# First block: the column groups of the modulation issued together, scores on a head's own rows, values of two heads at once, a split step-size weight

## The chip, the core and the metric

The program runs on one core of one Trainium2 chip. The metric is device time in microseconds, the median of several runs. The core has TensorE (PE, matmuls, with its weight loads listed apart as PEld), VectorE (DVE), ScalarE (ACT), GpSimd (POOL) and SyncE (SP), which here only issues DMA loads. Each engine works through its own instruction list in order; semaphores tie the lists together.

## The reference, cut to what matters

Two transformer blocks follow each other, each with a mixture of experts. The change lies in the first block alone. There a conditioning vector makes shifts, scales and gates (the modulation), and four mixers work beside each other on 256 tokens (and 256 context tokens): neighbourhood attention, a gated delta rule in both directions, differential attention and a Fourier mix.

```python
m_lat = jnp.split((s_lat @ w_mod[l] + b_mod[l])[:, None, :], 6, axis=-1)
h_lat = modulate(rmsnorm(x_lat, norm1_g[l]), m_lat[0], m_lat[1])
...
(na_q, na_k, na_v, dn_qkv, dn_a, dn_b, dn_gate, df_q, df_k, df_v, ft_u) = split_proj(h_lat @ w_in)
...
def diff_core(q, k, v, lam):
    s = jnp.einsum('bqhmd,bkhmd->bhmqk', q, k).astype(F32) * q.shape[-1] ** -0.5
    p = jax.nn.softmax(s, axis=-1)
    a = p[:, :, 0] - lam * p[:, :, 1]
    return jnp.einsum('bhqk,bkhd->bqhd', a, v.astype(F32))
...
x_lat = x_lat + m_lat[2] * (mix_lat @ w_out[l])
x_lat = x_lat + m_lat[5] * expert_choice_ffn(h_lat, w_router[l], w_gate[l], w_up[l], w_down[l])
```

Four heads of differential attention have two score maps each, over 32 features a map; a head's values have 64 features. `dn_a` and `dn_b` are the delta rule's step sizes, 16 columns of `w_in`. The second block has a modulation weight of its own, `w_mod_2`, which depends on no token and is worked off in the first block.

## The kernel before, in words

**Order.** A tile framework decides at build time in which order each engine's list stands; a generator `yield`s an estimate of the work it has just written. `beside(a, b, share)` mixes two generators, `weave(chain, fill)` writes a serial chain with another generator's pieces in between. A scheduler then places instructions by priorities and readiness, so the order of a list is not that of the code.

**Stages of the first block.** 1. The norm and the first 2048 columns of the modulation (`mods`, set 0). 2. Projections, the step sizes (`abp`, `abt`), the convolutions and the decay factors. 3. `solve()`, a triangular solve on DVE, one row of X after another, and woven into it the rest of the projections (`pj`, three fp32r products of high and low halves each) beside `mods` sets 1 and 2 of `w_mod`. What is left of that fill after the solve goes on alone. 4. `delta()`, the delta rule over 16 steps (state products `pa`, `oi`, `pb`, and `uw` for each new pair of steps), with `neighbours()`, `difference()`, `fourier()` and the three sets of `w_mod_2` woven in. 5. What is left of these, then the out-projection `pw` with `w_out`, router and experts.

**Modulation.** `mods` loads eight chunks of 1 MB of a set (tile `wmod`, from `S.load`'s ring of four buffers; 11 more are there once pool `main` is closed). For each it issues four matmuls with a 32-column stationary, each on its own column group, so that four groups fill the array. Their sums stand in one PSUM tile `mp` of its own pool. With `beside=8`, as in set 2 of `w_mod`, the eight chunks are summed by DVE in `macc` (L539, L541) instead, and four matmuls with ones finish it.

**Scores and values.** `scores(i)` in `difference()` makes two score tiles `ds` with K = 128: a padded copy `dqz` of the queries holds each map's 32 rows and zeros elsewhere. Maximum on DVE, exponential on ACT, the second map is scaled and added on DVE, the result scaled on POOL (`pr`). `transposes` turns it on PE (`pT`), and `pv` multiplies with a head's values, 64 columns of the array, four steps of the keys (`po`). Scores, values, `dfp` and `fp` share a pool of three PSUM banks (tag "mm"). An f32 matmul leaves two records in the trace, an fp32r one leaves one.

**Loads.** All weights come through SP's list, in order: the 24 chunks of `w_mod_2`, four loads of `w_out`, then the experts' `w_gate`, `w_up`, `w_down` in turn, as ring buffers come free. The expert stage reads 384 such loads of 1 MB.

Of the kernel before, what the change touches and what calls it, by code (L numbers as in the profile page):

```python
# [482 lines left out]
def block1(S):  # L483
# [45 lines left out]
    def mods(w, t, modT, bmod, cols, beside=0):  # L529
# [4 lines left out]
        for k in range(8):  # L534
# [9 lines left out]
            for j in range(4):  # L544
                mm(mp[32 * j:32 * j + 32, :], sc[:, k, :], wt[:, 512 * j:512 * j + 512], k == beside, k == 7 and not beside)
# [321 lines left out]
    fill = beside(projections(), chain_of([mods(I["w_mod"], 1, S.modT, V("b_mod"), (0,)), mods(I["w_mod"], 2, S.modT, V("b_mod"), (0,), 8)]), 3.5)  # L867
# [136 lines left out]
    def pv(P, e, u_, v):  # L1004
        r = slice(64 * e, 64 * e + 64)
        po = ps.tile([128, 512], F32, name="po", tag="mm")
        for kc in range(4):
            mm(po[r, 0:256], v[:, kc, 128 * P + 64 * e:128 * P + 64 * e + 64], PT[u_][:, kc, :], kc == 0, kc == 3)
        return po[r, 0:256]

    def attend(scores, values):
        for i in range(8 + 2):
            if i < 8:
                yield from scores(i)
            if 0 <= i - 1 < 8:
                transposes((i - 1) // 2, (i - 1) % 2)
                yield 0.5
            if i >= 3 and i % 2:
                values((i - 3) // 2)
                yield 1.0  # L1020

    def neighbours():
# [20 lines left out]
        def values(u_):  # L1043
            P, e = u_ // 2, u_ % 2
            r = slice(64 * e, 64 * e + 64)
            S.split(mix[0][r, P, :], mix[1][r, P, :], pv(P, e, u_, nv))
# [3 lines left out]
    def difference():  # L1050
# [10 lines left out]
        dqz, o = {}, {}  # L1061

        def scores(i):
            P, e, cc = i // 4, i // 2 % 2, i % 2
            if i % 4 == 0:
                dqz[P] = late.tile([128, 4, 256], F32, name="dqz", tag="q4", bufs=4)
                nc.vector.memset(dqz[P], 0.0)
                for j in range(4):
# [24 lines left out]
        def values(u_):  # L1093
            P, e = u_ // 2, u_ % 2
            r = slice(64 * e, 64 * e + 64)
            if e == 0:
                o[P] = late.tile([128, 256], F32, name="dfo", tag="t1", bufs=3)
            nc.scalar.copy(o[P][r], pv(P, e, u_, dv))
            if e == 1:
                sq = late.tile([128, 256], F32, name="dfsq", tag="t1", bufs=3)  # L1100
                nc.gpsimd.tensor_tensor(sq, o[P], o[P], op=ALU.mult)
                p = ps.tile([128, 512], F32, name="dfp", tag="mm")
                mm(p[:, 0:256], C("BD64"), sq)
                S.rsqrt(sq, p[:, 0:256], 1.0 / 64)
                nc.vector.scalar_tensor_tensor(o[P], o[P], gg, sq, op0=ALU.mult, op1=ALU.mult)
                S.split(mix[0][:, 4 + P, :], mix[1][:, 4 + P, :], o[P])
# [877 lines left out]
```

## Time and profile before

| what | value |
| --- | --- |
| median of 3 runs | 2150.25 us (2148.17 to 2151.69) |
| the profiled execution | 2152.28 us, its span 2150.1 us |
| PE busy | 1766.6 us (82%), 10570 matmuls |
| DVE, ACT, POOL busy | 710.8, 442.8, 216.2 us |
| HBM read | 720.96 MB, 336 GB/s over the span |
| chain that ended last | PE 41%, DMA 41%, DVE 8% |

The chain is followed back from the last instruction, at each step to what released it, so its shares tell which engine or transfer the end waited for; busy shares alone do not, as an engine may be busy beside another that is waited for. The first block ends where the expert stream begins, at about 380 us.

### The profile page before, as it was taken

How to read it: one execution, taken by the hardware profiler on the slowest of the kernel's cores; microseconds unless marked ns; L12 is line 12 of the kernel's file. 1: busy time of each engine (PE TensorE's matmuls, PEld its weight loads, DVE VectorE, ACT ScalarE, POOL GpSimd, SP SyncE). 2: the span in 40 equal slices, each digit the busy share in tenths (PEclk: the TensorE clock that was granted, in tenths of full speed). 3: DMA queues.
4: the chain of work that ended last, by engine and by line, in shares of the span. 5: the costliest groups of instructions: out<-in, count | busy, mean ns of one | idle time of the engine just before them, and what ended most of it. 6: DMA issues, size and time to landing. Idle time of an engine off the chain costs nothing.

```text
span 2150.1 us, 26014 instructions
## 1 busy us (share of the span) xinstructions
PE 1766.6 (82%) x10570; PEld 852.3 (40%) x10570; DVE 710.8 (33%) x1417; ACT 442.8 (21%) x791; POOL 216.2 (10%) x277
## 2 busy tenths in 40 slices
PE   6969998877666677677666678999998999999997
PEld 1647557411211112111211116899993433333333
DVE  4797673310001101111100115996552222222222
ACT  3623234200000001000100004676441111110111
POOL 2325422000000000000000002332020000000000
PEclk8989999786877777777887778999998999999998
DMA  7356559799999999999999996345587999999980
GB/s 307 129 196 255 195 205 407 312 424 424 424 424 425 425 424 425 425 424 424 424 425 424 423 422 243 125 158 229 182 308 290 417 410 386 398 392 384 398 331 21
DMA packets 120844, 723.76 MB, mean 337 GB/s; under 512 B 11456, under 2 KB 13248, under 8 KB 50448
## 3 DMA queue, kind: packets, MB, share of 16 engines
q1 hardware_dynamic: 119600, 717.97, 82.4%
q0 software_dynamic: 1120, 4.08, 0.5%
q8 instruction: 85, 1.39, 0.2%
q14 instruction: 39, 0.32, 0.0%
HBM read 720.96 MB, written 1.05 MB: 336 GB/s over the span
## 4 chain that ended last, share of the span: by engine, by line
PE 41%; DMA 41%; DVE 8%; issue 5%; ACT 3%; POOL 1%; SPq 0%; DVEq 0%; ACTq 0%; POOLq 0%
DMA w_up<-in_w_up_dram 14%; DMA w_gate<-in_w_gate_dram 13%; DMA w_down<-in_w_down_dram 12%; PE pj L253 7%; PE G L1729 6%; PE Yp L1729 6%; PE pw L253 2%; PE cmb L1729 2%; PE gx L370 2%; PE U L1729 2%; PE U L1179 2%; DVE tmp L781 1%; PE mp L514 1%; PE ya L253 1%; DMA w<-in_w_dram 1%
## 5 line engine op out<-in xcount | busy, mean ns | idle before, releaser
L1179 PE MATMUL U<-w_up,xg 128*32 128x512 f32 x1024 | 201.3, 875 | 99.5 <-DMA w_up<-in_w_up_dram 99.5
L1179 PE MATMUL Yp<-w_down,hT 128*32 128x512 f32 x1024 | 173.7, 786 | 84.6 <-DMA w_down<-in_w_down_dram 74.3
L1179 PE MATMUL G<-w_gate,xg 128*32 128x512 f32 x1024 | 162.8, 668 | 53.9 <-DMA w_gate<-in_w_gate_dram 53.6
L1285 DVE TENSOR_TENSOR hs<-hs,U 128x512 f32<-128x512 f32 x16 | 11.0, 688 | 469.6 <-PE U L1179 469.6
L1729 PE MATMUL Yp<-w,hT 128*64 128x512 f32 x512 | 136.3, 602 | 4.1 <-DVE hT L228 4.1
L1729 PE MATMUL G<-w,xg 128*64 128x512 f32 x512 | 138.5, 602 | 0.0
L1179 PEld LDWEIGHTS U<-w_up,xg 128*32 128x32 f32 x1024 | 25.0, 127 | 272.5 <-DMA w_up<-in_w_up_dram 240.3
L1729 PE MATMUL U<-w,xg 128*64 128x512 f32 x512 | 122.1, 592 | 0.0
L253 PE MATMUL pj<-uh,whi 128*128 128x256 f32 x408 | 118.2, 291 | 3.2 <-ACT uh L1409 3.2
L253 PE MATMUL pj<-uh,wlo 128*128 128x256 f32 x408 | 116.8, 286 | 1.1 <-DVE wlo L235 1.1
L253 PE MATMUL pj<-ul,whi 128*128 128x256 f32 x408 | 115.8, 284 | 0.0
L1179 PEld LDWEIGHTS Yp<-w_down,hT 128*32 128x32 f32 x1024 | 26.5, 124 | 207.1 <-DMA w_down<-in_w_down_dram 174.1
L1299 ACT COPY ys<-Yp 128x256 f32<-128x256 f32 x17 | 6.3, 372 | 480.6 <-DVE ys L1298 480.6
L234 ACT CAST whi<-win 128x1024 fp32r<-128x1024 f32 x72 | 75.0, 1046 | 97.8 <-PE pj L253 63.8
L1179 PE MATMUL cmb<-seln,ys 128*128 128x256 f32 x256 | 85.0, 467 | 11.7 <-DVE ys L1298 9.5
L1422 POOL DMA_DIRECT2D dist<-in_dist_dram x1 | 0.6, 606 | 910.7 <-PE tq L436 910.7
L1179 PEld LDWEIGHTS G<-w_gate,xg 128*32 128x32 f32 x1024 | 27.8, 114 | 150.6 <-DMA w_gate<-in_w_gate_dram 108.0
L1298 DVE COPY ys<-Yp 128x256 f32<-128x256 f32 x17 | 7.2, 425 | 242.2 <-PE Yp L1179 242.2
L1295 DVE SCALAR_TENSOR_TENSOR x<-cmb,modT,x 128x256 f32<-128x256 f32 x128 | 59.4, 483 | 68.0 <-PE cmb L1179 68.0
L253 PEld LDWEIGHTS pj<-uh,whi 128*128 128x128 f32 x408 | 77.6, 191 | 5.2 <-ACT uh L1409 3.5
L1179 PEld LDWEIGHTS cmb<-seln,ys 128*128 128x128 f32 x256 | 49.6, 218 | 75.6 <-DVE ys L1298 29.2
L253 PEld LDWEIGHTS pj<-uh,wlo 128*128 128x128 f32 x408 | 77.6, 190 | 2.5 <-DVE wlo L235 1.5
(565 smaller groups left out, 2986.2 us busy)
## 6 DMA issues: line engine op xcount, KB each, us to landing
w<-in_w_dram SPq DMA_DIRECT2D x192, 1024.0 KB, 8.4
w_gate<-in_w_gate_dram SPq DMA_DIRECT2D x128, 1024.0 KB, 19.6
w_up<-in_w_up_dram SPq DMA_DIRECT2D x128, 1024.0 KB, 19.6
w_down<-in_w_down_dram SPq DMA_DIRECT2D x128, 1024.0 KB, 19.6
wmod<-in_w_mod_dram SPq DMA_DIRECT2D x48, 1024.0 KB, 6.1
win<-in_w_in_dram SPq DMA_DIRECT2D x36, 1024.0 KB, 4.9
wout<-in_w_out_dram SPq DMA_DIRECT2D x8, 1024.0 KB, 5.8
wrnn<-in_w_rnn_out_dram SPq DMA_DIRECT2D x8, 640.0 KB, 7.3
```

Of the source, the lines that this page charges most:

```text
L234: self.nc.scalar.copy(hi, x)
L253: self.nc.tensor.matmul(out, a(k), b(k), start=(n == 0), stop=(n == 3 * K - 1))
L370: nc.tensor.matmul(q, xt[i % 2][:, i // 2, 128 * k:128 * k + 128], oh[:, i // 2], start=(i == 0), stop=(i == 3))
L514: nc.tensor.matmul(out, l, r, start=a, stop=b)
L781: nc.vector.tensor_tensor(tv, X[:, 0:i, 0:i], bc(Lt[:, None, 0:i, i], [128, i, i]), op=ALU.mult)
L1179: nc.tensor.matmul(out, l, r, start=a, stop=b)
L1285: nc.vector.tensor_tensor(hs, hs, U, op=ALU.mult)
L1295: nc.vector.scalar_tensor_tensor(x1[:, k, :], pc, S.modT[:, 40 + k, 0:1], x1[:, k, :], op0=ALU.mult, op1=ALU.add)
L1298: nc.vector.tensor_copy(ys[:, 0:256], Y[:, 0:256])
L1299: nc.scalar.copy(ys[:, 256:512], Y[:, 256:512])
L1422: nc.gpsimd.dma_start(dist, I["dist"])
L1729: nc.tensor.matmul(o, l, r, start=a, stop=b)
```

## The change

Five edits, all in the first block. `together` issues a list of matmuls and asks the scheduler to keep all after the first right behind it; `mods` uses it for a chunk's four column groups. Set 2 of `w_mod` loses `beside=8`, so PE works its chunks too. The step-size weight is split in high and low halves, 64 columns of fp32r, 16 single-pass matmuls. The scores of differential attention multiply the 32 rows of a map by the same 32 rows of the keys, both maps of a head issued together in two PSUM tiles, and `dqz` is gone. `pv` makes two heads at once on two column halves, so `values` comes once per pair, ahead of that step's transposes.

```diff
+    def together(self, L):
+
+        for i, (o, l, r, a, b) in enumerate(L):
+            if i == 0:
+                self.nc.tensor.matmul(o, l, r, start=a, stop=b)
+                continue
+            with self.tc.high_priority():
+                self.tc.keep_in_program_order(self.nc.tensor.matmul(o, l, r, start=a, stop=b))
...
-            for j in range(4):
-                mm(mp[32 * j:32 * j + 32, :], sc[:, k, :], wt[:, 512 * j:512 * j + 512], k == beside, k == 7 and not beside)
+            S.together([(mp[32 * j:32 * j + 32, :], sc[:, k, :], wt[:, 512 * j:512 * j + 512], k == beside, k == 7 and not beside) for j in range(4)])
...
+    wabs = he.tile([128, 8, 64], F32R, name="wabs")
+    S.split(wabs[:, :, 0:32], wabs[:, :, 32:64], wab)
     for k in range(8):
-        j = k % 4
         for i, h in enumerate(H):
-            mm(abp[32 * j:32 * j + 32, :], wab[:, k, :], h[:, k, :].bitcast(F32), k < 4 and i == 0, k >= 4 and i == 1)
+            mm(abp[0:64, :], wabs[:, k, :], h[:, k, :], k == 0 and i == 0, k == 7 and i == 1)
...
-    fill = beside(projections(), chain_of([mods(I["w_mod"], 1, S.modT, V("b_mod"), (0,)), mods(I["w_mod"], 2, S.modT, V("b_mod"), (0,), 8)]), 3.5)
+    fill = beside(projections(), chain_of([mods(I["w_mod"], 1, S.modT, V("b_mod"), (0,)), mods(I["w_mod"], 2, S.modT, V("b_mod"), (0,))]), 3.5)
...
-    def pv(P, e, u_, v):
-        r = slice(64 * e, 64 * e + 64)
+    def pv(P, v):
+
         po = ps.tile([128, 512], F32, name="po", tag="mm")
         for kc in range(4):
-            mm(po[r, 0:256], v[:, kc, 128 * P + 64 * e:128 * P + 64 * e + 64], PT[u_][:, kc, :], kc == 0, kc == 3)
-        return po[r, 0:256]
+            S.together([(po[64 * e:64 * e + 64, 0:256], v[:, kc, 128 * P + 64 * e:128 * P + 64 * e + 64], PT[2 * P + e][:, kc, :], kc == 0, kc == 3) for e in range(2)])
+        return po[:, 0:256]
 
     def attend(scores, values):
         for i in range(8 + 2):
             if i < 8:
                 yield from scores(i)
+            if i in (5, 9):
+                values((i - 5) // 4)
+                yield 1.0
             if 0 <= i - 1 < 8:
                 transposes((i - 1) // 2, (i - 1) % 2)
                 yield 0.5
-            if i >= 3 and i % 2:
-                values((i - 3) // 2)
-                yield 1.0
...
-            if i % 4 == 0:
-                dqz[P] = late.tile([128, 4, 256], F32, name="dqz", tag="q4", bufs=4)
-                nc.vector.memset(dqz[P], 0.0)
-                for j in range(4):
-                    r = slice(32 * j, 32 * j + 32)
-                    nc.scalar.copy(dqz[P][r, j, :], dq[r, P, :])
             prs, sums = [], []
-            for m in range(2):
-                p = ps.tile([128, 512], F32, name="ds", tag="mm")
-                mm(p, dqz[P][:, 2 * e + m, 128 * cc:128 * cc + 128], dk[:, P, :])
+            pp = [ps.tile([128, 512], F32, name="ds", tag="mm") for _ in range(2)]
+            S.together([(p, dq[r, P, 128 * cc:128 * cc + 128], dk[r, P, :], True, True) for p, r in ((pp[m], slice(64 * e + 32 * m, 64 * e + 32 * m + 32)) for m in range(2))])
+            for p in pp:
...
-                yield 0.9
+                yield 0.6
```

**The order after the solve.** On DVE, before, at the solve's last two rows (`tmp` and `X` are the solve's, `Y` its transposed result, `vfm` the copy that the PE transposes `tk` read):

```order
L782 TENSOR_REDUCE X<-tmp 128x30
L539 TENSOR_SCALAR macc<-wmod,sc 128x2048
L781 TENSOR_TENSOR tmp<-X,Lt 128x961
L228 COPY vfm<-pj 128x512
L782 TENSOR_REDUCE X<-tmp 128x31
L235 TENSOR_TENSOR wlo<-win,whi 128x1024
L786 STREAM_TRANSPOSE Y_1219<-X 128x1024
L788 STREAM_TRANSPOSE Y_1221<-X 128x1024
L541 SCALAR_TENSOR_TENSOR macc<-wmod,sc,macc 128x2048
L228 COPY vfm<-pj 128x512
```

and now:

```order
L791 TENSOR_REDUCE X<-tmp 128x30
L790 TENSOR_TENSOR tmp<-X,Lt 128x961
L791 TENSOR_REDUCE X<-tmp 128x31
L795 STREAM_TRANSPOSE Y_1222<-X 128x1024
L228 COPY vfm<-pj 128x512
L797 STREAM_TRANSPOSE Y_1224<-X 128x1024
L235 TENSOR_TENSOR wlo<-win,whi 128x1024
L228 COPY vfm<-pj 128x512
```

The macc rows are gone, and the first copy vfm stands behind the last X and one Y instead of ahead of both.

On PE, before, at the second `tk` behind the solve (pj are projections of 512 tokens):

```order
L253 MATMUL pj<-hl,whi 128x512
L253 MATMUL pj<-hh,wlo 128x512
L639 MATMUL tk<-cst,vfm 128x128 x4
L253 MATMUL pj<-hh,whi 128x512
L253 MATMUL pj<-hl,whi 128x512
L253 MATMUL pj<-hh,wlo 128x512
```

and now:

```order
L253 MATMUL pj<-hl,whi 128x512
L253 MATMUL pj<-hh,wlo 128x512
L563 MATMUL tq<-cst,ms 128x128 x4
L260 MATMUL mp<-wmod,sc 32x512
L263 MATMUL mp<-wmod,sc 32x512 x3
L647 MATMUL tk<-cst,vfm 128x128 x4
L253 MATMUL pj<-hh,whi 128x512
L253 MATMUL pj<-hl,whi 128x512
```

A chunk's four matmuls of the modulation now stand between the projections; there are eight such groups from the solve to the first `uw`, and before only the four matmuls on macc and ones.

**The order at the scores.** On PE, before, in the delta rule's late steps (pa, oi and pb are its state products):

```order
L514 MATMUL ds<-dk,dqz 128x512
L514 MATMUL pa<-S_1653,wT 32x128 x2
L514 MATMUL oi<-S_1653,qn 32x128 x2
L514 MATMUL ds<-dk,dqz 128x512
L514 MATMUL pa<-S_1655,wT 32x128 x2
L514 MATMUL oi<-S_1655,qn 32x128 x2
L514 MATMUL pb<-u,kd 64x64 x4
L514 MATMUL ds<-dk,dqz 128x512
```

and now, at the second and third pair:

```order
L260 MATMUL ds<-dk,dq 128x512
L263 MATMUL ds<-dk,dq 128x512
L523 MATMUL pb<-u,kd 64x64 x8
L260 MATMUL ds<-dk,dq 128x512
L523 MATMUL pa<-S_1676,wT 32x128 x2
L523 MATMUL pa<-S_1678,wT 32x128 x2
L523 MATMUL oi<-S_1676,qn 32x128 x2
L523 MATMUL oi<-S_1678,qn 32x128 x2
L260 MATMUL mp<-wmod,sc 32x512
L263 MATMUL mp<-wmod,sc 32x512
L263 MATMUL ds<-dk,dq 128x512
L263 MATMUL mp<-wmod,sc 32x512 x2
```

The second pair's two scores stand next to each other, the third pair's have state products and half a chunk of the modulation between them; three of the eight pairs stand together in the whole list, and all sixteen scores stand ahead of the last pb, where before five came after it.

**The order ahead of the out-projection.** On PE, before, up to the first pw (fp is the Fourier mix, tq a transpose of the modulation, bw a router product):

```order
L1001 MATMUL pT<-cst,pr 128x128 x4
L514 MATMUL mp<-wmod,sc 32x512 x7
L1001 MATMUL pT<-cst,pr 128x128 x4
L555 MATMUL tq<-cst,ms 128x128 x4
L514 MATMUL po<-PT,dv 64x256 x4
L555 MATMUL tq<-cst,ms 128x128 x4
L514 MATMUL dfp<-dfsq,bd_103 128x256
L514 MATMUL fp<-fc,fu 128x256 x4
L514 MATMUL fp<-tim,fy 128x256 x8
L514 MATMUL fp<-fz,fc 128x256 x4
L278 MATMUL bw_3052<-wr,modT 128x16 x8
L253 MATMUL pw<-mixh,whi 128x256
```

and now:

```order
L523 MATMUL fp<-tim,fy 128x256 x7
L523 MATMUL fp<-fz,fc 128x256 x4
L563 MATMUL tq<-cst,ms 128x128 x4
L260 MATMUL mp<-wmod,sc 32x512
L263 MATMUL mp<-wmod,sc 32x512 x3
L260 MATMUL mp<-wmod,sc 32x512
L263 MATMUL mp<-wmod,sc 32x512 x3
L260 MATMUL mp<-wmod,sc 32x512
L263 MATMUL mp<-wmod,sc 32x512 x3
L287 MATMUL bw_3052<-wr,modT 128x16 x8
L563 MATMUL tq<-cst,ms 128x128 x4
L253 MATMUL pw<-mixh,whi 128x256
```

Scores, values and most transposes have left this place, three chunks of the modulation stand in it, ahead of bw, and the first products of pw use the high half whi alone.

## Rows read from the trace of the kernel before

**Rows 1.** The page's chain that ended last, by line:

```profile
DMA w_up<-in_w_up_dram 14%; DMA w_gate<-in_w_gate_dram 13%; DMA w_down<-in_w_down_dram 12%; PE pj L253 7%; PE G L1729 6%; PE Yp L1729 6%; PE pw L253 2%; PE cmb L1729 2%; PE gx L370 2%; PE U L1729 2%; PE U L1179 2%; DVE tmp L781 1%; PE mp L514 1%; PE ya L253 1%; DMA w<-in_w_dram 1%
```

**Rows 2.** Windows: us, busy of PE, PEld, DVE, ACT, POOL, clock, DMA share, GB/s.

```profile
380.00:385.00 5.00, 3.65 (x16) 3.54 (x16) 3.81 (x15) 0.38 (x1) 2.50 (x8) 0.50 0.16 63
385.00:390.00 5.00, 5.00 (x19) 2.18 (x19) 1.78 (x12) 2.35 (x5) 2.05 (x6) 0.50 0.00 0
390.00:395.00 5.00, 5.00 (x23) 2.63 (x20) 0.31 (x1) 1.66 (x2) 0.00 (x0) 0.50 0.61 202
395.00:400.00 5.00, 5.00 (x34) 1.55 (x38) 0.31 (x1) 0.00 (x0) 0.00 (x0) 0.69 0.87 294
400.00:405.00 5.00, 5.00 (x52) 1.44 (x48) 0.00 (x0) 0.60 (x1) 0.00 (x0) 1.00 1.02 352
```

**Rows 3.** Timeline of SP's queue: start, us, DMAs issued.

```profile
326.92 8.55 SPq L216 DMA_DIRECT2D w_gate<-in_w_gate_dram  x8
```

**Rows 4.** Chain of waits, 145 to 205 us: start, us, piece, instructions.

```profile
153.29 1.19 DVE macc L539
...
180.47 10.53 PE pj L253 x46
191.01 0.97 PE mp L514 x2
```

**Rows 5.** Timeline of PE, the transposes that wait for vfm.

```profile
156.84 1.11 PE L639 MATMUL tk<-cst,vfm 128*128 128x128 f32 x4 [2.90 <-DVE vfm L228]
...
176.02 0.66 PE L639 MATMUL tk<-cst,vfm 128*128 128x128 f32 x4 [0.80 <-DVE vfm L228]
```

**Rows 6.** Windows of the delta rule and of the stretch behind it.

```profile
205.00:301.00 96.00, 95.56 (x943) 51.87 (x942) 68.17 (x188) 28.12 (x72) 42.05 (x86) 1.00 0.52 185
301.10:342.00 40.90, 35.77 (x319) 20.75 (x318) 22.46 (x59) 21.04 (x40) 8.55 (x11) 1.00 0.86 336
```

**Rows 7.** Chain of waits, 300 to 400 us.

```profile
307.43 1.89 PE po L514 x8
...
340.49 1.69 PE bw L278 x16
342.18 5.84 PE pw L253 x48
```

**Rows 8.** Chain of waits, 40 to 90 us.

```profile
54.38 1.85 PE abp L514 x10
...
61.84 1.04 ACT whi L234
...
71.16 1.28 ACT L617
...
76.56 2.44 POOL wlo L235
```

**Rows 9.** Timeline of DVE at the solve's end.

```profile
156.70 1.15 DVE L782 TENSOR_REDUCE X<-tmp 128x31 f32<-128x961 f32 x1
...
158.90 2.00 DVE L786 STREAM_TRANSPOSE Y<-X 128x1024 f32<-128x1024 f32 x1
160.81 1.21 DVE L788 STREAM_TRANSPOSE Y<-X 128x1024 f32<-128x1024 f32 x1
```

**Rows 10.** Groups of DVE, 157 to 205 us: busy, mean ns, idle before.

```profile
L541 DVE SCALAR_TENSOR_TENSOR macc<-wmod,sc,macc 128x2048 f32<-128x2048 f32 x7 | 18.4, 2634 | 0.1
```

**Rows 11.** Groups of PE, 205.07 to 301.1 us.

```profile
L514 PE MATMUL ds<-dk,dqz 128*128 128x512 f32 x24 | 13.3, 636 | 0.0
...
L1001 PE MATMUL pT<-cst,pr 128*128 128x128 f32 x48 | 7.9, 282 | 0.0
```

**Rows 12.** The page's DMA issues: KB each, median us to landing.

```profile
wout<-in_w_out_dram SPq DMA_DIRECT2D x8, 1024.0 KB, 5.8
```

**Rows 13.** Instructions on tile ds: ns min/median/max.

```profile
L1080 ACT ACTIVATE pr<-ds,mx x16: 671/688/698, 262.4 to 322.9; 128x512 f32<-128x512 f32 x16
```

More of the change, by code (lines that the diff above doesn't have):

```diff
@@ L648, in block1 @@
     abp = pc.tile([128, 512], F32, name="abp", tag="ch")
+    wabs = he.tile([128, 8, 64], F32R, name="wabs")
+    S.split(wabs[:, :, 0:32], wabs[:, :, 32:64], wab)
     for k in range(8):
-        j = k % 4
         for i, h in enumerate(H):
-            mm(abp[32 * j:32 * j + 32, :], wab[:, k, :], h[:, k, :].bitcast(F32), k < 4 and i == 0, k >= 4 and i == 1)
+            mm(abp[0:64, :], wabs[:, k, :], h[:, k, :], k == 0 and i == 0, k == 7 and i == 1)
     abT = sb.tile([128, 512], F32, name="abT", tag="T2", bufs=2)
-    nc.scalar.copy(abT, abp)
+    nc.scalar.copy(abT[0:64, :], abp[0:64, :])
     ka.append(conv(wk, 1, 3, 512))
@@ L657, in block1 @@
     for t in range(4):
-        mm(abt[:, 16 * t:16 * t + 16], abT[:, 128 * t:128 * t + 128], C("sel32")[:, 0:16])
+        mm(abt[:, 16 * t:16 * t + 16], abT[0:64, 128 * t:128 * t + 128], C("sel32")[0:64, 0:16])
     ab = sm.tile([128, 4, 16], F32, name="ab")
@@ L1041, in scores, with values @@
             yield 0.9
[L1043 to L1046, printed above, removed]
+        def values(P):
+            S.split(mix[0][:, P, :], mix[1][:, P, :], pv(P, nv))
         yield from attend(scores, values)
@@ L1060, in difference @@
         nc.vector.tensor_scalar(gg, V("df_g"), 1.0 - lam_init, None, op0=ALU.mult)
-        dqz, o = {}, {}
         def scores(i):
             P, e, cc = i // 4, i // 2 % 2, i % 2
-            if i % 4 == 0:
-                dqz[P] = late.tile([128, 4, 256], F32, name="dqz", tag="q4", bufs=4)
-                nc.vector.memset(dqz[P], 0.0)
-                for j in range(4):
-                    r = slice(32 * j, 32 * j + 32)
-                    nc.scalar.copy(dqz[P][r, j, :], dq[r, P, :])
             prs, sums = [], []
-            for m in range(2):
-                p = ps.tile([128, 512], F32, name="ds", tag="mm")
-                mm(p, dqz[P][:, 2 * e + m, 128 * cc:128 * cc + 128], dk[:, P, :])
+            pp = [ps.tile([128, 512], F32, name="ds", tag="mm") for _ in range(2)]
+            S.together([(p, dq[r, P, 128 * cc:128 * cc + 128], dk[r, P, :], True, True) for p, r in ((pp[m], slice(64 * e + 32 * m, 64 * e + 32 * m + 32)) for m in range(2))])
+            for p in pp:
                 mx = sm.tile([128, 1], F32, name="mx", bufs=6)
@@ L1091, in scores, with values @@
             PR[i // 2, cc] = prs[0]
[L1093 to L1106, printed above, removed]
+        def values(P):
+            o = late.tile([128, 256], F32, name="dfo", tag="t1", bufs=3)
+            nc.scalar.copy(o, pv(P, dv))
+            sq = late.tile([128, 256], F32, name="dfsq", tag="t1", bufs=3)
+            nc.gpsimd.tensor_tensor(sq, o, o, op=ALU.mult)
+            p = ps.tile([128, 512], F32, name="dfp", tag="mm")
+            mm(p[:, 0:256], C("BD64"), sq)
+            S.rsqrt(sq, p[:, 0:256], 1.0 / 64)
+            nc.vector.scalar_tensor_tensor(o, o, gg, sq, op0=ALU.mult, op1=ALU.mult)
+            S.split(mix[0][:, 4 + P, :], mix[1][:, 4 + P, :], o)
         yield from attend(scores, values)
```

## The prediction

> **What bounds the kernel now.** I began with the page's chain of waits [rows 1]: its largest pieces are the DMA of the first block's expert weights, and TensorE (PE) comes after them with projections (pj). So a microsecond saved in the first block counts only if it reaches the point where the expert stream runs. The table of windows shows that point [rows 2]: from 380 to 405 us the DMA moves 63, 0, 202, 294 and 352 GB/s where the stream afterwards moves 424. That is (1-63/424)x5 + 5 + (1-202/424)x5 + (1-294/424)x5 + (1-352/424)x5 = 14.3 us of lost DMA time. The ring of loads is full then, and no expert's product has yet freed a buffer. An earlier start of the experts' products closes this gap, one for one, up to 14.3 us less whatever the stream itself starts later; its first load is issued at 326.92 [rows 3]. From 405 us on the stream is bound by DMA and the change touches nothing.
>
> Then I followed the first block backwards in three stages. From the solve to the delta rule (156.8 to 205 us) the chain is PE on projections, released by VectorE (DVE) [rows 4, 5]. From 205 to 301 us PE is busy 95.56 of 96 us [rows 6]: PE work alone counts. From 301.1 us (T0: the last state products pa) to the out-projection pw at 342.18 [rows 7], PE is busy 35.77 of 40.90 us [rows 6], so 5.1 us are waits. The working is made against the profiled execution, 2152.28 us (span 2150.1), which is 2.0 us above the median of 2150.25.
>
> **The change, stage by stage.**
>
> *Up to the solve's end.* Five f32 matmuls of the step size stood on the chain with 1.85 us [rows 8]. Single-pass ones are priced like a projection of the same width, 10.53/46 = 0.23 us [rows 4]: -0.7. ScalarE's order has one change of function table less, 1.28 us [rows 8]. Against that GpSimd's order has one wlo (2.44 us, [rows 8]) ahead of the decay factors that it did not have there. The stage moves by -2.0 to +0.4; I take the middle, -0.8. At the solve's end the 1.19 us macc goes [rows 4], but the last X reduction and the first transpose Y now stand ahead of the copy vfm for which PE waits 2.90 us [rows 5]; they take 1.15 and, as the two Y show, 1.21 to 2.00 [rows 9]: 2.4 to 3.1, less what records of one engine overlap, +2.6 (2.0 to 3.1). Together +0.6 (-1.2 to +2.3).
>
> *156.8 to 205 us.* PE gains eight groups of four column-group matmuls; a group side by side costs what the chain shows, 0.97 us [rows 4]: +7.8. It loses the products of macc with ones, which stand in two pieces of 0.97 each: -1.9. By the order three projections less stand here, -0.7, and the second wait for vfm, 0.80 us behind a macc [rows 5], goes. Sum +4.4. The DVE work that goes is 18.4 us [rows 10], but all of it except that wait lay beside a PE that was busy: it bought nothing on this path. This term is a loss, and the surest of all.
>
> *205 us to T0.* Counted on PE from the two orders. Modulation: 65 matmuls in 18 runs, 22 slots of at most four, become 68 in 20 slots, as three groups are still cut by a score: -1.9. Values: 20 matmuls at 1.89/4 = 0.47 us [rows 7] become 24 in 14 slots: -2.8. Scores: 12 at 13.3/12 = 1.1 us [rows 11] become 16, of which only three pairs stand next to each other: 13 slots if a pair runs side by side, +1.1, and 16 if not, +4.4. Eight more transposes at 7.9/48 [rows 11]: +1.3. One dfp (256 columns in f32, like a value): +0.5. Sum -1.8. The padding's memsets and copies were not waited for, so they count for nothing. A pair takes two of the three "mm" banks at once, and PE had no slack to wait in: +1.5 for new waits (0 to 4). Sum -0.3 (-1.8 to +5.5). T0 moves by 0.6 + 4.4 - 0.3 = +4.7.
>
> For the side-by-side pair a page gives a figure. The Trainium skill, "TensorE: Matmul & The Clock Gate", Part 3, has row tiles of 32 rows and 512 columns running concurrently, four of them 3.07 times as fast as in turn. No row of this trace has two 512-column products on different rows; by that figure the scores' term is +1.1 as I took it, without it +4.4.
>
> *T0 to the out-projection.* All scores are now done before T0, so the tail loses four (-4.4), eight transposes (-1.3), one dfp (-0.5); values go from 12 slots to 5 (-3.3), modulation from 9 slots to 7 (-1.9). PE work: 35.8 - 11.4 = 24.4. The out-projection's first weight cannot come sooner than this: its load takes the buffer of modulation chunk 22, whose products now stand ahead of two more groups (1.9), a transpose (0.7) and bw (1.69, [rows 7]), so at T0 + 20.1 + waits; then 5.8 us to land [rows 12] and 1.04 for its high half whi [rows 8]. With 3 of the 5.1 us of waits kept, pw starts at T0 + 29.9 instead of T0 + 41: -11.0 (-8.9 with all of the waits, -14.0 with none). The first pw rows in the new order use whi alone, so no wlo is waited for.
>
> *The experts.* The first expert load stands behind the four out-projection loads, which now follow chunk 24's group: T0 + 24.4 - 2.4 + 3 = T0 + 25.0, before 326.92 - 301.1 = 25.8. The stream starts 4.7 - 0.8 = 3.9 us later, and the gap lets up to 14.3 - 3.9 = 10.4 us through. The sum, 4.7 - 11.0 = -6.3, fits. 2152.28 - 6.3 = 2146.0; from the median **2144.0 us**.
>
> **Rivals.** 0.2% (4.3 us) is about what a measurement of this kernel can tell from no change.
>
> *A, deeper.* No new waits before T0 (-1.8 instead of -0.3) and one instead of three us in the tail: -1.5 - 2.0 on top, -9.8, about 2140.5. For it: DVE has 18.4 us less to do, PE is the engine all wait for, and the DMA gap is wide enough (the stream then starts 0.4 later, 13.9). Against: orders with more work packed in front of T0 have more places to wait.
>
> *B, no change that can be told.* The few pairs do not run side by side (+3.3) and the tail keeps its 5.1 us of waits (+2.1): -0.9, about 2149. For it: ten of the sixteen scores stand singly in any case, and the tail's end is a serial chain over four engines.
>
> *C, slower.* Score pairs hold two of three banks until both exponentials have read them: the product 1.1, two exponentials of 0.69 and a maximum before each [rows 11, 13], some 3 us in which one bank serves values and the other scores. PE stands in a fixed order, so a wait for a bank stops the delta rule's products behind it, and with them everything up to T0. Eight pairs at w us each: the gain is gone at w = 6.3/8 = 0.8, and the kernel is slower by more than 0.2% from w = 10.6/8 = 1.3. With w = 1.8 the sum is -6.3 - 1.5 + 14.4 = +6.6, about 2157. Against: other work stands between most pairs and their next use.
>
> The page that speaks for C: the Trainium skill, "TensorEngine Tiling (Array Packing)", Gotcha 1 (PSUM Pressure), says that row tiles write to different PSUM banks and so raise the pressure on them. By it the banks and not PE's work decide the stage, which is C's sum; the trace shows only 0.4 us of PE idle there with each score's bank taken by itself [rows 6], and nothing yet of two.
>
> **How the numbers follow.** The forecast, -4.3 to -8.5, gets 0.44; A 0.14; B, everything within 4.3, 0.27; C 0.15. Faster 0.58, same 0.27, slower 0.15. The predicted time is the forecast's. The sums of the terms' good and bad ends run from -12.6 (early stage and tail at their best) to about +3.3 (solve +2.3, products not side by side and 4 us of waits, tail with 5.1): from the median 2137.5 to 2153.5. Range 2137 to 2153; it leaves out most of C.
>
> **What would show it.** Delta's first uw at about 210 us instead of 205 shows the 4.4 and the 0.6. PE nearly without idle time from there to T0 (about 306) confirms -0.3; idle time ended by ScalarE's exponential or DVE's maximum is C. A pw start 30 us behind T0, with the last wait ended by whi, confirms the tail. The windows around 380 to 405 us should show about half to two thirds of the 14.3 us gone: if the gap is as wide as before, something other than the products of the first experts opens it, and the forecast is wrong at that step. A shift of T0 by more than 10 would also make it wrong.

## The result, and the profile after

The changed kernel takes 2163.45 us (median of 5 runs, 2159.83 to 2167.91), the kernel before beside it 2150.25 (2147.28 to 2151.83): a ratio of 1.0058, 95% interval 1.0044 to 1.0072. It is slower, by some 13 us, where 6 us less were forecast. The profiled execution is one of its fastest, span 2158.2 us against 2150.1, so its trace shows 8.1 of the 13 us.

| point in the profiled execution, us | before | after | moved | forecast |
| --- | --- | --- | --- | --- |
| first copy vfm starts (end of the solve) | 156.1 | 159.0 | +2.9 | +0.6 |
| first uw (delta rule) | 205.0 | 211.6 | +6.6 | +5.0 |
| T0 (last step's state products begin) | 301.1 | 318.5 | +17.4 | +4.7 |
| first pw (out-projection) | 342.0 | 348.7 | +6.7 | -6.3 |
| first expert load issued | 326.9 | 345.0 | +18.1 | +3.9 |

In the changed kernel the last step's products pa stand in two places, at 318.50 and 322.05 us, one for each direction; T0 is the first of them. What leaves the forecast most is one stage: from the first uw to T0 it takes 106.9 us instead of 96.0. The tail behind it is as short as forecast, 30.2 us, so pw starts no later than the early stages alone would make it; the first expert load stands behind the out-projection's loads and moves with T0. The windows of the two stages (columns as in [rows 6]) show both:

```profile
211.60:318.50 106.90, 101.69 (x975) 53.35 (x975) 76.05 (x208) 31.88 (x78) 43.20 (x88) 0.94 0.51 179
318.50:348.70 30.20, 27.01 (x290) 16.68 (x285) 13.20 (x40) 12.13 (x22) 4.66 (x7) 0.99 0.71 264
```

PE was busy 95.56 of 96 us there [rows 6]; now it idles for 5.2 us, 4.8 more, and its mean granted clock is 0.94, not 1.00, which as an estimate costs (1 - 0.94) x 106.9 = 6.4 us. Together that is 11.2, beside the 10.9 by which the stage is longer. The waits of PE in that stretch (engine, line, released by: us in total, times, longest):

```profile
PE pb L523 <- ACT u L912: 2.8, 1, 2.8
PE pb L523 <- DVE u L939: 0.9, 1, 0.9
PE pa L523 <- DVE S L963: 0.7, 1, 0.7
PE pT L1010 <- POOL pr L1048: 0.7, 1, 0.7
```

Windows of 4 us at the stops, and behind them, show the clock:

```profile
218.00:222.00 4.00, 0.93 (x10) 0.34 (x8) 2.94 (x9) 1.04 (x3) 2.21 (x5) 0.95 0.95 374
222.00:226.00 4.00, 3.59 (x18) 2.16 (x19) 3.20 (x8) 0.92 (x3) 1.84 (x4) 0.50 0.15 59
226.00:230.00 4.00, 4.00 (x27) 1.25 (x27) 1.23 (x5) 0.64 (x2) 0.47 (x2) 0.70 0.69 231
...
262.00:266.00 4.00, 3.27 (x31) 1.45 (x29) 3.35 (x10) 0.88 (x3) 0.57 (x2) 0.99 0.00 0
266.00:270.00 4.00, 4.00 (x22) 2.06 (x22) 3.75 (x11) 1.40 (x4) 1.88 (x4) 0.58 0.02 4
...
306.00:310.00 4.00, 3.00 (x26) 1.51 (x22) 2.74 (x7) 1.36 (x3) 0.94 (x2) 1.00 0.54 221
310.00:314.00 4.00, 4.00 (x24) 2.25 (x25) 3.19 (x8) 0.78 (x2) 1.33 (x4) 0.57 0.02 4
```

Three times PE stops, for 3.5, 0.7 and 0.9 us by the list of waits, and then works on almost without a gap in windows whose clock is 0.50 to 0.70, so for part of the time or all of it at the lower of its two levels (0.50 is 1.2 GHz). What DVE waits for in front of the first stop and of the third (timeline of DVE):

```profile
218.93 0.43 DVE L1041 TENSOR_TENSOR ns<-ns,nab 128x256 f32<-128x256 f32 x1 [3.13 <-DMA nab<-in_na_bias_dram]
...
307.07 0.48 DVE L1100 SCALAR_TENSOR_TENSOR dfo<-dfo,gg,dfsq 128x256 f32<-128x256 f32 x1 [1.33 <-ACT dfsq L268]
```

At 218 us the bias table nab of the neighbourhood attention is late: its loads land after 7.1 and 8.8 us, before the change after 4.1 and 6.9. ScalarE waits for the maximum behind that addition, and its copy of u, for which PE waits, stands behind that (218.93, 219.40, 220.12 and 220.80 us). The second stop is taken up with e15 below. At 307 us DVE stands in its list at the norm of the first pair of differential heads, whose values now come at once and early, and waits for ScalarE; the delta rule's u stands behind it.

The stream's gap, answering [rows 2], is smaller but begins later:

```profile
395.00:400.00 5.00, 5.00 (x19) 2.14 (x17) 1.25 (x7) 1.67 (x3) 1.26 (x3) 0.50 0.77 313
400.00:405.00 5.00, 5.00 (x24) 2.96 (x28) 0.57 (x2) 1.67 (x2) 0.00 (x0) 0.50 0.62 228
405.00:410.00 5.00, 5.00 (x32) 1.18 (x28) 0.04 (x1) 0.00 (x0) 0.00 (x0) 0.57 0.93 344
410.00:415.00 5.00, 5.00 (x52) 1.37 (x48) 0.00 (x0) 0.60 (x1) 0.00 (x0) 1.00 1.01 372
```

By the prediction's formula that is 1.3 + 2.3 + 0.9 + 0.6 = 5.2 us lost instead of 14.3. The stream starts 18.1 us later ([rows 3] against the row below, SP's queue) and gets 9.1 back: 9.0, beside 8.1 between the spans. The experts' first products G do not start earlier, as the prediction had it, but 9.2 us later (394.3 us, before 385.1); the gap is smaller because the stream moves by more than they do.

```profile
344.97 7.90 SPq L216 DMA_DIRECT2D w_gate<-in_w_gate_dram  x8
```

### The profile page after: what moved, and what is told of

The parts are those of the page before. It is cut to its first block, busy times and chain, and to the rows that moved or that the text cites. A ratio compares the mean times of both kernels' runs of the same rounds, so it can differ in the third digit from the quotient of the medians.

```text
span 2158.2 us, 26066 instructions
## 1 busy us (share of the span) xinstructions
PE 1766.9 (82%) x10610; PEld 855.4 (40%) x10610; DVE 691.6 (32%) x1406; ACT 438.8 (20%) x779; POOL 214.7 (10%) x277
## 4 chain that ended last, share of the span: by engine, by line
PE 41%; DMA 41%; DVE 8%; issue 5%; ACT 2%; POOL 1%; SPq 0%; DVEq 0%; ACTq 0%; POOLq 0%
DMA w_up<-in_w_up_dram 14%; DMA w_down<-in_w_down_dram 13%; DMA w_gate<-in_w_gate_dram 12%; PE pj L253 7%; PE G L1724 6%; PE Yp L1724 6%; PE pw L253 2%; PE cmb L1724 2%; PE gx L379 2%; PE U L1724 2%; PE U L1174 1%; DVE tmp L790 1%; PE ya L253 1%; PE mp L260 1%; DMA w<-in_w_dram 1%
## 5 line engine op out<-in xcount | busy, mean ns | idle before, releaser
L1724 PE MATMUL G<-w,xg 128*64 128x512 f32 x512 | 138.6, 602 | 0.0
L1174 PEld LDWEIGHTS Yp<-w_down,hT 128*32 128x32 f32 x1024 | 26.5, 124 | 206.9 <-DMA w_down<-in_w_down_dram 174.1
L1174 PE MATMUL cmb<-seln,ys 128*128 128x256 f32 x256 | 87.6, 481 | 11.2 <-DVE ys L1293 9.5
```

The lines of the kernel that those rows point to most:

```text
L1174: nc.tensor.matmul(out, l, r, start=a, stop=b)
L1724: nc.tensor.matmul(o, l, r, start=a, stop=b)
```

## The experiments

Times are medians, each ratio is to the kernel before run beside it. "uw" is the start of the first uw and "Fu-pw" the time from it to the first pw, both in one profiled execution (Fu-pw is 137.0 before, 137.1 after). A difference of 2 or 3 us between two rows lies within their intervals.

| run | what | us | ratio to before (95%) | uw | Fu-pw |
| --- | --- | --- | --- | --- | --- |
| e1 | change, bias table early | 2165.06 | 1.0065 (1.0047 to 1.0083) | 218.1 | 134.3 |
| e2 | change, first norm late | 2161.63 | 1.0049 (1.0032 to 1.0066) | 217.8 | 137.2 |
| e3 | change, macc back | 2154.35 | 1.0024 (1.0012 to 1.0036) | 209.9 | 137.1 |
| e4 | change, padded scores | 2153.69 | 1.0018 (1.0005 to 1.0030) | 211.8 | 129.7 |
| e5 | change, step size in f32 | 2159.70 | 1.0037 (1.0025 to 1.0049) | 211.3 | 137.6 |
| e6 | change, one score tile | 2161.77 | 1.0049 (1.0033 to 1.0064) | 216.5 | 137.0 |
| e8 | change, single values | 2162.68 | 1.0053 (1.0038 to 1.0068) | 215.8 | 136.6 |
| e17 | before + groups | 2149.95 | 0.9993 (0.9983 to 1.0002) | 203.8 | 137.3 |
| e7 | before + groups + values | 2140.12 | 0.9947 (0.9934 to 0.9961) | 203.7 | 126.9 |
| e9 | e7 + score pairs | 2150.33 | 1.0006 (0.9995 to 1.0017) | 201.5 | 132.6 |
| e10 | e7 + early tables | 2145.14 | 0.9972 (0.9960 to 0.9984) | 203.3 | 134.3 |
| e11 | e7 + step size split | 2144.93 | 0.9975 (0.9965 to 0.9984) | 209.8 | 126.8 |
| e12 | e7 + set 2 on PE | 2147.25 | 0.9986 (0.9976 to 0.9995) | 206.9 | 129.7 |
| e13 | e7 + 32 rows only | 2140.52 | 0.9954 (0.9939 to 0.9969) | 202.6 | 127.3 |
| e14 | e7 + pairs, tables late | 2150.31 | 0.9998 (0.9988 to 1.0007) | 202.8 | 138.6 |
| e15 | e14 at 0.9 | 2146.56 | 0.9982 (0.9966 to 0.9997) | 204.5 | 135.7 |
| e16 | e7 at 0.6 | 2138.03 | 0.9936 (0.9919 to 0.9954) | 204.0 | 122.4 |

Theory 1, at the start, is that single stops of PE and the clock behind them cost the time. Theory 2, its rival, is that score pairs hold two of three PSUM banks.

**Two stops taken out: e1 and e2.**

```diff
     weave(solve(), fill)
+    nab0 = sb.tile([128, 2, 2, 256], F32, name="nab", tag="D")
+    nc.gpsimd.dma_start(nab0, I["na_bias"].rearrange("p (c h k) -> p c h k", c=2, h=4)[:, :, 0:2, :])
...
-            if i % 4 == 0:
+            if i == 0:
+                bias[P] = nab0
+            if i == 4:
                 bias[P] = late.tile([128, 2, 2, 256], F32, name="nab", tag="q4", bufs=4)
```

> The changed kernel, with one edit: the first half of the neighbourhood attention's bias table is loaded right behind the solve into a tile that is free by then, instead of at the start of the delta rule. Theory 1 (stops and clock): in the delta stage PE stands still at about 218 us because this table lands 7.1 us after its issue instead of 4.1, and then runs some 6 us at a granted clock near 0.5 to 0.66; without it the last pa starts about 6 us earlier than 318.5 and the time falls by about 6 us against the changed kernel (about 2157). Theory 2 (score pairs hold two of three PSUM banks): the stop moves to another place, the time stays within 2 us of 2163.

```diff
         def values(P):
             o = late.tile([128, 256], F32, name="dfo", tag="t1", bufs=3)
             nc.scalar.copy(o, pv(P, dv))
+            od2.append(o)
+            for P, o in enumerate(od2 if P else []):
-            sq = late.tile([128, 256], F32, name="dfsq", tag="t1", bufs=3)
+                sq = late.tile([128, 256], F32, name="dfsq", tag="t1", bufs=3)
```

> The changed kernel, with the norm of the first pair of differential heads (square, product with BD64, two exponent functions with their table loads, scaling, split) written behind the second pair's values instead of between the delta rule's steps. Theory 1: the stop of PE at about 307 us, where DVE stands in its list before the scaling that waits for ScalarE and the delta rule's u stands behind it, goes with its half-clock time: 2 to 4 us less than the changed kernel, unless the norm now lengthens the tail. Theory 2: no change within 2 us.

Neither gave its forecast: 2165.06 and 2161.63. In e1 the wait for u goes, but the transposes then wait 1.5 us for pr, and from first uw to pw only 2.8 us are won. In e2 the stage before the last pa is shorter and the tail longer by as much (PE waits 3.3 us for dfsq there), which its expectation had as the exception. Both also have a first uw 6 us later than the profiled change, which neither edit touches: a second loss, ahead of the solve, whose first row of X starts at 103.0 and 104.2 us there and at 98.7 in the profiled change. Theory 1 in the form "remove one stop, win its price" falls.

**One edit of the change undone: e3, e4, e5, e6, e8.** e3, e4, e5 and e8 put the lines of the diff shown above back, one edit each. e6 keeps the unpadded rows, one tile at a time:

```diff
-            pp = [ps.tile([128, 512], F32, name="ds", tag="mm") for _ in range(2)]
-            S.together([(p, dq[r, P, 128 * cc:128 * cc + 128], dk[r, P, :], True, True) for p, r in ((pp[m], slice(64 * e + 32 * m, 64 * e + 32 * m + 32)) for m in range(2))])
-            for p in pp:
+            for m in range(2):
+                r = slice(64 * e + 32 * m, 64 * e + 32 * m + 32)
+                p = ps.tile([128, 512], F32, name="ds", tag="mm")
+                mm(p, dq[r, P, 128 * cc:128 * cc + 128], dk[r, P, :])
...
-                yield 0.6
+                yield 0.9
```

> The changed kernel, with beside=8 for set 2 of the first modulation weight put back: DVE sums its eight chunks again. Theory 1 with the prediction's term: PE loses eight groups between the solve and the first uw (4.4 us, uw at about 207 instead of 211.6), the loads of the second weight's first chunks come earlier, the bias table no longer lands among them, and the first stop goes as well: 8 to 11 us less than the changed kernel (about 2153). If only the groups count: 4 us less. If neither counts and the time is set by the score pairs: within 2 us of 2163.

> The changed kernel, with the padded scores put back (dqz, K = 128, one PSUM tile at a time, 0.9 yielded). Theory 1: the padding's two buffers hold the Fourier mix's tables back as before the change, so the bias table shares the DMA with 0.9 MB less and lands earlier: the first stop shrinks by about 2 us and the time by 2 to 4. Theory 2: the banks are free again, all stops between 255 and 315 us go, and the time falls by 5 us or more, with the stop at 218 left as it is.

> The changed kernel with the step-size weight as before (f32, four column groups, no split). Theory A: the single-pass products leave PE idle while its granted clock is low (in the changed kernel PE is busy 7.18 of the 10 us from 40 us on at a clock of 0.63, in e1 6.60 at 0.50 with the last of these products at 58.3 us instead of 54.0; in the kernel before 9.23 at 0.84), so the projections behind run at the low clock for longer, in some executions more than in others. Then the first uw comes 1 to 6 us earlier and the median falls by 2 to 4 us to about 2160. Rival: the spread comes from the first loads (the last product of modulation set 0 starts between 33.6 and 35.9 us); then the median moves by less than 1.5 us.

> The changed kernel with unpadded 32-row scores, but one PSUM tile taken and one product issued at a time, 0.9 yielded, as before the change. From the first uw to pw the changed kernel takes 137.2 us and e4 with padded scores 129.7. Theory 2 (two of three banks taken at once): this kernel comes to 130 to 132 us there and to about 2155. If the 32-row products themselves cost it, or the Fourier tables that come early where the padding is gone: 134 to 137 us, and 2160 to 2163.

> The changed kernel with values of one head at a time, as before. By the prediction's term of PE work, some 18 slots of 0.47 us come back, of which about 10 stand ahead of pw: 3 to 5 us more than the changed kernel, about 2167. Rival: the pair's late and bunched values, and the norm behind them, are themselves a cause of the stops between 255 and 310 us; then the time falls by 2 us or more.

Putting back DVE's sums gives 9.1 us, padded scores 9.8, the f32 step size 3.8; one tile at a time 1.7, single values 0.8, the last two within the noise. e3 has the size that was expected, but not for the reason: the stops are still there (Fu-pw 137.1), and its experts' first products start 4.2 us earlier where its pw starts 1.7 earlier. e4 is the one that takes out the last two stops; 0.9 us of the first is left, and the clock stays at 1.00. In e8 the clock is at 1.00 from 232 to 320 us and the time hardly moves. e6 surprised: the stage has lost the pairs and not the low clock, and behind its first stop PE is at 0.50 a second time, without a gap in its work (windows of PE and the others):

```profile
286.00:290.00 4.00, 4.00 (x35) 2.13 (x30) 2.37 (x9) 1.45 (x4) 0.39 (x1) 1.00 0.98 408
...
292.00:304.00 12.00, 12.00 (x69) 6.18 (x69) 7.45 (x23) 0.78 (x3) 2.78 (x6) 0.50 0.00 1
```

That made Theory 3: products on 32 rows let the clock fall by themselves.

**Building up from before: e17, e7, and one more edit at a time, e9, e11, e12.** e17 has `together` in `mods` alone, e7 also the new `pv`, `attend` and `values`.

> The kernel before with the column groups of the modulation kept together and nothing else. e7 (groups and values) is 10.2 us faster than before, from the first uw to pw 126.9 us instead of 137.0. By the prediction's terms the groups bring 1.9 + 1.9 us of PE work there and the values 2.8 + 3.3: this kernel then takes about 133 us there and 2146 in all. If the groups bring nearly all: 127 to 129 us, about 2141. If the values bring nearly all: 136 us, 2149 to 2150.

> The kernel before with two of the five edits only: column groups of the modulation kept together, and values of two heads at once. If the three other edits are what costs: first uw at 205 us as before, first uw to pw about 130 us instead of 137, so about 6 us less than before, 2143 to 2146. If the gain of e4 came from something that the early stage's shift brought with it: within 2 us of 2150.

> e7 (groups and values only, 2140.1 us) plus the change's unpadded score pairs. What the scores edit costs by itself. Theory 1 (stops): the Fourier tables come early, the bias table late, PE stops at the delta rule's start and twice later, each time with some us at a low clock: 2147 to 2152, PE's clock below 0.97 from the first uw to the last pa. Theory 3 (e6: the clock fell to 0.50 at about 290 us with PE busy without a gap): products on 32 rows let the granted clock fall also without a stop; the same time, but low-clock stretches with PE busy all through. If the scores edit is harmless without the other two: 2138 to 2142.

> e7 plus the single-pass step-size weight. Theory A: PE is less busy while its clock is low at 30 to 55 us, the last of these products starts 1 to 4 us later, the solve starts later: 1 to 5 us more than e7 (2141 to 2145) with a wider spread. Prediction's term: 1 us less than e7.

> e7 plus set 2 of the first modulation weight on PE instead of DVE. Prediction's term, 4.4 us more up to the first uw plus 2 for vfm behind X and Y: 2144 to 2147. Rival: the expert stream's gap, still open in e7, takes part of it, or DVE's relief gives some back: 2140 to 2142.

The groups alone change nothing that can be told (ratio 0.9993), with the values the kernel is 10 us faster than before; the values without the groups were not run. In e7 the delta stage is as long as before and the tail 10 us shorter, at full clock:

```profile
203.70:300.00 96.30, 96.07 (x993) 50.38 (x992) 72.43 (x199) 32.93 (x81) 44.75 (x88) 1.00 0.63 235
300.00:330.60 30.60, 26.52 (x271) 16.64 (x269) 16.61 (x47) 15.92 (x29) 7.21 (x9) 1.00 0.72 281
```

Each further edit costs: scores +10.2, step size +4.8, set 2 on PE +7.1. With e7's 2140.1 that adds up to 2162.2, beside 2163.45 measured for all of them together, and undoing each from the other side gives 22.7 us (9.8, 3.8 and 9.1): the three account for the result. The values do not add up so: put in with the groups they bring 10 us, taken out of the change they cost nothing that can be told (e8).

The step size: in e7, with f32 products, PE and its clock come back like this (windows from 38 us),

```profile
38.00:42.00 4.00, 3.34 (x6) 0.55 (x6) 3.23 (x8) 3.56 (x7) 3.69 (x5) 0.50 1.02 424
42.00:46.00 4.00, 3.78 (x14) 0.91 (x13) 3.40 (x9) 3.03 (x6) 3.08 (x4) 0.77 0.66 277
46.00:50.00 4.00, 3.87 (x13) 1.52 (x11) 3.62 (x7) 1.47 (x3) 2.29 (x4) 1.00 0.01 2
```

and in e11, with single-pass products, like this:

```profile
38.00:42.00 4.00, 1.86 (x4) 0.47 (x3) 3.08 (x10) 3.41 (x7) 3.33 (x5) 0.50 1.02 424
42.00:46.00 4.00, 2.23 (x5) 0.96 (x6) 3.62 (x10) 2.66 (x5) 2.85 (x5) 0.50 0.74 309
46.00:50.00 4.00, 3.16 (x8) 1.61 (x7) 3.62 (x9) 1.53 (x2) 2.29 (x4) 0.50 0.00 0
50.00:54.00 4.00, 4.00 (x11) 3.13 (x10) 2.25 (x5) 0.60 (x1) 1.42 (x2) 0.50 0.40 98
```

The same products, done faster, leave PE idle while it waits for the split activations, and the clock returns some 10 us later (at about 54 us instead of 44), with projections behind it. The times differ between executions, yet the two kinds lie apart: full clock comes to stay by 46 us at the latest in every trace with f32 products, and between 47 and 55 us in every one with single-pass products; the solve's first row of X starts at 95.9 to 99.0 us in the former and at 98.4 to 104.2 in the latter. That these two go together is read from the traces and not tried apart. In e11 the delay is hidden by a wait, and replaced by another: in its chain the wlo on GpSimd stands between the two rows of decay factors, and everything of the solve comes after (start, us, piece).

```profile
82.85 1.84 POOL egl L721 x4
...
84.76 2.77 POOL wlo L235
87.53 1.04 POOL rE L724
```

**Inside the scores edit: e10, e13 to e16.** Of e10 the edit is the padding's buffer, `tag="dqz", bufs=1` instead of `tag="q4", bufs=4`. e13 changes the operands, but for the last product of each pair of heads, and leaves e7's order as it is:

```diff
+                r = slice(64 * e + 32 * m, 64 * e + 32 * m + 32)
+                if i % 4 == 3 and m == 1:
+                    mm(p, dqz[P][:, 2 * e + m, 128 * cc:128 * cc + 128], dk[:, P, :])
+                else:
+                    mm(p, dq[r, P, 128 * cc:128 * cc + 128], dk[r, P, :])
-                mm(p, dqz[P][:, 2 * e + m, 128 * cc:128 * cc + 128], dk[:, P, :])
```

e14 has the change's pairs with the padding still made and read by the same last product; e15 is e14 with `yield 0.9`, e16 is e7 with `yield 0.6`.

> e7 with padded scores as it has them, but the padding in one buffer of its own, so that the Fourier tables find free buffers and are loaded at the delta rule's start as in the changed kernel. Theory 1: the stop at the first bias addition is back, with its low clock: 5 to 8 us more than e7 (about 2146). Theory 3: the padded products keep the clock up: at most 3 us more than e7 (about 2142).

> e7, in its order of instructions, with 14 of the 16 score products on 32 rows of unpadded queries and keys; the padding is still made, and the last product of each pair of heads still reads it, so buffers and loads are as in e7. Theory 3 (32-row products let the clock fall): clock below 0.97 between first uw and last pa, 3 us or more above e7's 2140.1. If the rows don't matter: 2138 to 2142, clock 1.00 there as in e7.

> e7 with the change's score pairs (two PSUM tiles at once, two products together, 0.6 yielded), the padding still made and read once per pair of heads, so that the Fourier tables stay late. The scores edit without its early tables: by e9 less e10 5 us above e7, about 2145, with stops of PE ended by DVE's S and u between 250 and 300 us and low clock behind them. If early tables are all that the scores edit costs: 2138 to 2142.

> e14 (pairs in two PSUM tiles) with 0.9 yielded per score instead of 0.6; 12 of the 16 scores then stand ahead of the last pb and 4 behind it, as in e7, where e14 has all 16 ahead. Pace theory: what costs e14 its 10 us over e7 is that 0.6 lets the weave put more of the scores' DVE and ScalarE work between the delta rule's steps; then this kernel is within 2 us of e7's 2140.1, with the clock at 1.00 from first uw to last pa. Pair theory (two banks at once, two maxima in a row on DVE): 2146 or more.

> e7 (padded scores, one tile at a time) with 0.6 yielded per score instead of 0.9; all 16 scores then stand ahead of the last pb. Pace theory: about 2148 to 2151, stops ended by DVE and low clock between 250 and 310 us. Pair theory: 2138 to 2142.

Theory 3 falls: e13 is e7 to 0.4 us, at full clock. What lowers the clock in e6 at 291 us, with no wait ahead of it in the trace, stays open.

```profile
202.60:299.30 96.70, 96.42 (x993) 50.08 (x992) 72.37 (x199) 32.89 (x81) 44.76 (x88) 1.00 0.63 233
```

The tables are a part of it: in e10 the first bias addition waits 3.9 us for nab (1.5 in e7), PE is busy 2.92 and 2.75 of two windows of 4 us and the next runs at 0.73:

```profile
208.00:212.00 4.00, 2.92 (x18) 1.35 (x17) 1.88 (x5) 1.23 (x4) 3.80 (x8) 1.00 0.99 351
212.00:216.00 4.00, 2.75 (x18) 1.28 (x17) 3.60 (x12) 0.78 (x2) 2.93 (x6) 0.84 0.42 162
216.00:220.00 4.00, 4.00 (x23) 1.37 (x21) 1.54 (x4) 0.78 (x2) 0.02 (x1) 0.73 0.78 260
```

e10's 5.0 us are not the tables' alone, though: with one buffer the second memset of dqz moves from 209.7 to 284.5 us and PE's order with it, and of the 7.4 us that e10's trace is longer than e7's from the first uw to pw only 3.0 lie ahead of the last uw. And the pairs with late tables (e14) cost as much as the whole scores edit, so the tables add nothing to them. The pace theory falls too: e16 with 0.6 and all sixteen scores ahead of the last pb has the lowest median of all, 2138.03, not clear of e7's. Pairs at the slow pace still cost 6.4 (e15). So the pair is enough to cost this much on e7; in the change itself, where the tables are early as well, undoing it alone gives only 1.7 (e6). e15's trace shows how little it takes. One stop, in the timelines of DVE and PE:

```profile
253.68 0.67 DVE L1085 TENSOR_REDUCE mx<-ds 128x1 f32<-128x512 f32 x1
254.28 0.73 DVE L1097 SCALAR_TENSOR_TENSOR pr<-pr,f 128x512 f32<-128x512 f32 x1
254.94 1.22 DVE L962 TENSOR_TENSOR S<-Sd,pb 64x128 f32<-64x128 f32 x4
...
255.67 0.90 PE L523 MATMUL pa<-S,wT 128*32 128x128 f32 x5 [0.74 <-DVE S L962]
```

and the windows from there:

```profile
252.00:256.00 4.00, 3.26 (x30) 1.50 (x26) 3.62 (x11) 0.57 (x3) 0.64 (x2) 1.00 0.02 9
256.00:260.00 4.00, 3.96 (x21) 1.55 (x19) 3.50 (x10) 1.56 (x4) 1.64 (x4) 0.58 0.00 0
260.00:264.00 4.00, 4.00 (x25) 1.43 (x24) 0.57 (x2) 0.00 (x0) 0.27 (x1) 0.50 0.18 27
264.00:268.00 4.00, 4.00 (x21) 2.01 (x22) 2.04 (x6) 0.00 (x0) 1.32 (x4) 0.50 0.61 240
268.00:272.00 4.00, 4.00 (x57) 2.20 (x53) 3.17 (x10) 0.13 (x1) 1.42 (x3) 0.71 0.28 59
```

With pairs, a maximum and the combination pr stand on DVE right ahead of the delta rule's S, 1.40 us; PE waits 0.74 for it and then runs 16 us below full clock: (0.42 + 0.50 + 0.50 + 0.29) x 4 = 6.8 us, an estimate, of the 8.8 us that this execution is longer than e7's from the first uw to pw. In e7 a maximum alone stands ahead of S there, and PE does not wait. The same stop (mx and pr ahead of S, PE waits 0.73 to 0.76 us) stands in the traces of the change, e1, e2, e3, e5, e9 and e14 too, and its price is not the same: 6.8 us of clock in e14, 1.7 in the change, e2, e3, e5 and e9, and nothing right behind it in e1:

```profile
264.00:268.00 4.00, 3.26 (x30) 1.51 (x26) 3.65 (x11) 0.55 (x3) 0.67 (x2) 1.00 0.00 0
268.00:272.00 4.00, 3.96 (x41) 1.49 (x38) 3.47 (x10) 1.70 (x5) 1.61 (x4) 1.00 0.02 4
```

So the wait is the pair's doing, and what the clock makes of it differs from execution to execution: e15's ten runs lie between 2139.99 and 2154.28 us. Nor does a longer wait always cost the clock: in e7's tail PE waits 1.8 us for mixh and the clock stays at 1.00:

```profile
320.00:324.00 4.00, 2.15 (x11) 1.60 (x10) 1.49 (x3) 3.85 (x6) 0.00 (x0) 1.00 1.01 422
```

Whether the two banks force DVE's list into this order, or only the two products issued together, was not tried; no wait of PE for a bank shows in it.

## Why the prediction was wrong, point by point

- **The step that failed: "+1.5 for new waits (0 to 4)" before T0.** PE idled for 4.8 us more than before, above the bound; what the sum had no term for was the lower clock around the stops, an estimated 6.4 us in the changed kernel. The stage's term of -0.3 came out at +10.9, more than the upper end of +5.5. By these estimates that leaves -0.3 us for the list of PE work, where -1.8 stood: about right. Put by edit, the forecast's sum was -9.9 for groups and values, +5.0 up to the first uw (step size and set 2) and -1.4 for the rest, the scores above all; measured were -10.1 (e7), +4.8 and +7.1 (e11, e12) and +10.2 (e9). So the scores missed by most, and the two early edits come next.
- **"The padding's memsets and copies count for nothing"** was right for the engines (e13 still makes them and is as fast as e7) and wrong for the buffers: the padding held two buffers back, and without it the Fourier tables are loaded on top of the bias table. That is a part of the 5.0 us of e10, and adds nothing where the pairs stand (e9 and e14, 2150.33 and 2150.31).
- **Up to the solve's end, +0.6.** It was +2.9 in the profiled execution, beyond the range's +2.3. The vfm term was about right: the last X and a Y of 1.94 us, issued at 157.13, stand ahead of the copy at 158.99. The step-size term had the right matmul time (five single-pass products, 1.16 us on the chain, -0.7) and the wrong sign: e11 costs 4.8 us. PE gets idle in a stretch at low clock, and GpSimd's wlo, taken as the bad end of a range, is what the chain goes through; no table load stands on that chain between 36 and 104 us, so its gain of 1.28 us was not there to be had.
- **From the solve to the first uw, +4.4:** 211.6 - 159.0 = 52.6 against 205.0 - 156.1 = 48.9, so +3.7. Set 2 on PE costs 7.1 us in all (e12): its first uw is 3.2 us later than e7's, and another 2.8 us go from there to pw, whose cause stays open. That DVE's 18.4 us bought nothing fits this.
- **The tail, pw at T0 + 29.9:** 30.2, with the last wait ended by wout's load and whi, as foretold (chain of waits):

```profile
342.84 4.74 DMA wout<-in_w_out_dram
...
347.65 2.00 ACT whi L234 x2
```

  The terms behind it were shared out wrongly, and that their sum held (9.9 forecast, 10.1 in e7) is in part luck. Groups and values were to bring 3.8 and 6.1 us of PE work; the groups alone bring nothing that can be told and a tail of 41.0 us (e17), with the values it is 30.6 (e7). In e17's tail PE is busy for 2.7 us less than the 35.77 of [rows 6], but idles for 7.9 us instead of 5.1:

```profile
300.10:341.10 41.00, 33.08 (x288) 20.70 (x285) 20.46 (x56) 20.32 (x38) 7.96 (x11) 0.96 0.71 273
```

- **The gap of the expert stream** closes by 9.1 of 14.3 us, within the half to two thirds that the prediction named, but by luck: it was to close by experts' products that start earlier, and they started 9.2 us later, behind a stream that started 18.1 us later.
- **Rival C** had the right side and named one of the three edits that cost, not the mechanism: PE waited for DVE's list, not for a bank, and not 1.3 us at each of eight pairs but once to three times, with the clock behind it.

The Trainium skill, "TensorE: Matmul & The Clock Gate", section "HAM oscillation", tells of a kernel in which waits for data let the clock fall, so that the work behind each starts cold. The traces here agree in part: behind the 0.74 us of waiting in e15 the clock falls to 0.50 and 6.8 us are lost, but behind the same wait in e1 it stays at 1.00, and in e6 it falls to 0.50 with no wait right ahead of it.

## What to carry to other kernels

Where PE's list is full, a wait of under a microsecond is not priced by its length (here it cost from nothing to 6.8 us of clock): look at the granted clock in the windows behind it, in more than one execution, and ask of each edit what it puts ahead of the instruction that the full engine waits for next. Work that goes away frees buffers, and loads that were held back by them start at once, on top of others. Five edits in one change can hide a good one: two of these together are worth 10 us, the other three cost 22 on top of them, and the version with the lowest median (e16, ratio 0.9936) keeps the padded scores, DVE's sums and the f32 step size.

## What the runs showed of the hardware that was not expected

PE's granted clock can stay at 0.50 for as long as 12 us with PE busy without a gap (e6, 292 to 304 us), and at 1.00 with PE busy for 2.15 of 4 us (e7, 320 to 324 us). Doing the same products in less time can cost time: PE's clock returned at about 44 us with slower f32 products and at about 54 us with single-pass ones (e7 and e11). Two score products on different rows, issued together, do run side by side: at 258.41 us of the changed kernel the first records of both start within 0.01 us, and each of the two records of a product takes 0.59 to 0.69 us there, where one record of a padded product alone takes 0.59 (median, e7). That is the prediction's +1.1 for pairs that stand together.
